# Unused strips at both ends of the partition, so that the large tiles of a transformer block begin at multiples of 256 bytes

## The chip, the cores and the metric

The kernel runs on one core of one Trainium2 chip. The metric is the device time of one execution in microseconds. The profile's span runs from the first to the last instruction of one profiled execution; the device time of a run is somewhat longer than such a span.

## The reference

One layer of a hybrid block over 1024 tokens of width 1024, all in float32: stick-breaking attention with 16 heads of 64, a gated short convolution beside it, a gated merge, and a SwiGLU channel layer with 2816 hidden columns.

```python
mod = silu(c) @ ada_w + ada_b                      # six vectors: sh1, sc1, g1, sh2, sc2, g2
h = rmsnorm(x, ln1_g) * (1 + sc1) + sh1
p = h @ w_in                                       # 1024 x 8192
q, k, v, cb, cc, cx, ga, gb = split(p)
q, k = rmsnorm(q, q_norm_g), rmsnorm(k, k_norm_g)  # per head
y_a = stick_breaking_attention(q, k, v)            # strictly causal, 128-query blocks
y_b = cb * causal_dwconv(cc * cx, conv_w)          # three taps
merged = sigmoid(ga) * (y_a @ w_branch_a) + sigmoid(gb) * (y_b @ w_branch_b)
x = x + g1 * (merged @ w_out)
h = rmsnorm(x, ln2_g) * (1 + sc2) + sh2
f = (silu(h @ w_ffn_gate) * (h @ w_ffn_up)) @ w_ffn_down
out = x + g2 * f
```

Stick-breaking attention: with z = q.k / 8, the weight of key s for query t is sigmoid(z_ts) times the product of 1 - sigmoid(z_tj) over s < j < t.

## The kernel before

Every float32 product is made of three matmuls of the type fp32r: each operand is split into a rounded part ("hi", made by ScalarE) and the rest ("lo", made by VectorE), and hi x hi, hi x lo and lo x hi are added up in PSUM. A matmul has one operand that is loaded into the array (the weights' side; row PEld of the profile) and one that is streamed through it. In the helper `half_prod` (L122 to L129), which makes most products, the weights' split `w` is loaded and the factor `fh`, `fl` is streamed, 512 columns of float32, so 2048 bytes in each partition:

```python
for k in range(4):
    nc.tensor.matmul(ps, wh[:, k, :], fh[:, k, :], start=(k == 0), stop=False)    # L127
    nc.tensor.matmul(ps, wh[:, k, :], fl[:, k, :], start=False, stop=False)       # L128
    nc.tensor.matmul(ps, wl[:, k, :], fh[:, k, :], start=False, stop=(k == 3))    # L129
```

So one product is 12 matmuls. The stages, in the order of time:

- Start (to about 70 us): `x` and its transpose `xts` are loaded, the first modulation is summed up on VectorE (`mod_sum`), and the normed input is split into the four `big` tiles. L290 in `mm_tok` makes v and k from them; here the weights' split is streamed. This lasts to about 165 us.
- Gates (165 to about 570 us): q, the convolution's inputs and the two gates are 20 groups ("gates") of 1024 x 256 columns. Each is one Strassen step: seven half products (`g_prod`), whose streamed factors 0 to 3 lie in `big` tiles and whose factors 4, 5 and 6 are the tiles `ft4`, `ft5` and `ft6`. GpSimd makes the sums of the weights (`ws`), and a generator (`mods_later`) sums the second modulation on VectorE beside the later gates.
- Attention (575 to about 1005 us): scores (L782, L783), sigmoid on ScalarE into `pt`, a scan on VectorE (L788), transposes (L803), and the product with the values' differences (L818, L819). A second generator (`fillers`) puts the products of the convolution branch between (L876 to L878, L895 to L897).
- Merge and output projection (1005 to about 1240 us): `w_branch_a` (L876 to L878 with `ya` streamed), then w_o (L1190 to L1192), where the weights' split `whi`, `wlo` is streamed. `preload_wo` brings five of the eight slices of the first half of w_o ahead, into the pool `wpx`.
- Hidden layer (1240 to about 1640 us): 11 groups, each one Strassen step for the gate and one for the up projection, 22 in all, with seven half products each. The streamed factors are `big` tiles and three pairs of own tiles: `rh2`/`rl2`, `rh6`/`rl6` and `rh3`/`rl3`. The results `c..` are split into `fs` and stored to `d_f`.
- Down projection (1640 us to the end): seven products again (`down`, L1410 to L1412), with the weights' split streamed; `f` is loaded back from `d_f`, and `g2b` and `xo` are loaded for the last sums.

Tiles lie in pools that are stacked from both ends of a partition: a pool with `side="right"` grows down from the far end, the others up from the near end. Pools are opened and closed by stage, so that a later stage's tiles lie where an earlier one's were. At the near end lie the constants; most constants have odd sizes, so the first large tile behind them begins 64 bytes past a multiple of 256, and since the tiles behind it are multiples of 256 bytes long, nearly all have that offset. At the far end the first pool holds `rq` and begins where the partition's usable space ends; nearly all of its followers lie 224 past a multiple of 256. In bytes from the start of the partition:

| tile | at, before | past 256 | past 64 |
|---|---|---|---|
| first of the four `big` | 22,080 | 64 | 0 |
| `ft6` | 112,192 | 64 | 0 |
| `whi`, `wlo` of the gates (first) | 104,000; 95,808 | 64 | 0 |
| `rh6`, `rl6`, `rh3`, `rl3` | 147,008 to 179,776 | 64 | 0 |
| `ft5`, `ft4` | 195,552; 211,936 | 224 | 32 |
| `rh2`, `rl2` | 212,960; 221,152 | 224 | 32 |
| preloaded w_o, `whi`, `wlo` | 207,840; 218,080 | 224 | 32 |
| `pt0` to `pt4` (attention) | 207,840 on | 224 | 32 |
| `c10` to `c31`, `fs` (hidden layer) | 184,288 on | 224 | 32 |
| `dm` (identity), `mk` (mask) | 16,512; 17,024 | 128 | 0 |

The order of instructions on each engine is the program's as the scheduler left it, in part fixed by added dependences (`in_order`, `issue_after`, `high_priority`). Waits between engines are derived from the tiles, including waits for the last user of the bytes in which a new tile comes to lie.

Of the kernel before, what the change touches and what calls it, by code (L numbers as in the profile page):

```python
# [8 lines left out]
F32 = mybir.dt.float32  # L9
# [7 lines left out]
P = 128  # L17
# [6 lines left out]
SECS = (2, 4, 3, 5)  # L24
NH = HID // P
EPS = 1e-6


def block_kernel(tc, x, x_t, cols, ada_1, ada_2, ada_row, w_q, w_kv, w_v1, w_cg, w_a, w_b, w_o, w_g, w_u, w_d, out):
    nc = tc.nc  # L30
    st = ExitStack()
    const = st.enter_context(tc.tile_pool(name="const", bufs=1, reuse_waits="tile"))
# [5 lines left out]
    def nm(s):  # L38
        uid[0] += 1
        return f"{s}_{uid[0]}"  # L40
# [65 lines left out]
    gcol = cst[:, 82:98].rearrange("p (m k) -> p m k", m=2)  # L106
    nc.vector.tensor_scalar(out=qgc, in0=qgc, scalar1=0.125, scalar2=None, op0=ALU.mult)
    mod = const.tile([P, 4, 8], F32, name="mod")
    rqs = ExitStack()
    rqp = rqs.enter_context(tc.tile_pool(name="rqp", bufs=1, side="right", reuse_waits="tile"))  # L110
    rq = rqp.tile([P, 2, 8, H], F32, name="rq")

    def rstd_of(ss, scale, pool, w, r=None, eng=nc.gpsimd):

        m = pool.tile([P, 8], F32, tag="rs_m", bufs=3, name=nm("rs_m"))
        if r is None:
            r = pool.tile([P, 8], F32, tag="rs_r", bufs=3, name=nm("rs_r"))[:, :w]
        eng.tensor_scalar(out=m[:, :w], in0=ss, scalar1=scale, scalar2=EPS, op0=ALU.mult, op1=ALU.add)  # L118
        nc.gpsimd.tensor_tensor(out=r, in0=m[:, :w], in1=nhalf[:, :w], op=ALU.pow)
# [466 lines left out]
    def end_q():  # L586
# [6 lines left out]
        for i in range(8):  # L593
            nc.tensor.transpose(tr[:, i * H:(i + 1) * H], ss[i // 4][:, i % 4 * P:(i % 4 + 1) * P], ident[:H, :H])
        ms = gp.tile([P, 8, H], F32, name="ms16")
        nc.vector.tensor_scalar(out=ms.rearrange("p i h -> p (i h)"), in0=tr[:, :8 * H], scalar1=1.0 / DH, scalar2=EPS,
                                op0=ALU.mult, op1=ALU.add)
# [416 lines left out]
    for n in range(2):  # L1014
        for k in range(KT):
            yr = fp.tile([P, 512], F32, tag="yr", bufs=2, name=nm("yr"))
            nc.sync.dma_start(yr, d_ya[n][:, k, :])
            tag, bufs = slots[n * KT + k]
# [564 lines left out]
```

## Time and profile before

| | us |
|---|---|
| median of 3 runs | 1853.54 |
| lowest, highest | 1847.68, 1854.77 |
| span of the profiled execution | 1845.0 |

The profiled execution's own device time is not told apart from the three; its span lies 2.7 us under the lowest and 8.5 us under the median of the runs. A row of a group names line, engine, operation, the written tile and the tiles read (the streamed one and the loaded one in a matmul, in the order of their names), the shape and the count; behind the bar follow the busy time, the mean duration of one in ns, and the idle time before them. In the timeline each row has the start and the duration in us.

### The profile page before, as it was taken

What the parts mean: (1) busy time and instruction counts of PE and PEld (TensorE: products, weight loads), DVE (VectorE), ACT (ScalarE), POOL (GpSimd) and SP (SyncE); (2) the same over time, 40 slices, a digit from 0 to 9 for tenths busy, and PEclk for the clock granted to TensorE, in tenths of its full rate; (3) what the DMA queues carried; (4) which work ended last, traced back from release to release, by engine and by line L of the source; (5) the groups of instructions that cost most, each with busy time, mean ns of one, the idle gap of its engine ahead of it and who ended that gap; (6) DMA issues with size and microseconds to landing.
All of it is one profiled execution on the core that took longest, in us unless ns stands there. A gap on an engine that the chain in (4) does not pass through costs nothing.

```text
span 1845.0 us, 24888 instructions
## 1 busy us (share of the span) xinstructions
PE 1810.0 (98%) x8829; PEld 1504.7 (82%) x8829; DVE 1346.3 (73%) x1948; ACT 792.1 (43%) x1494; POOL 369.1 (20%) x277
## 2 busy tenths in 40 slices
PE   7999999999999999999999999999999999999999
PEld 5787778888889988888888788877888888878887
DVE  6874776779873888888887644589877787644776
ACT  4352553333343656665665311664443344322321
POOL 1043327423230000000000000115544544200000
PEclk9999999999999999999999999999999999999999
DMA  9598452227748665678554636424533344299766
GB/s 389 196 311 299 166 186 86 80 75 247 273 164 250 158 194 170 188 227 282 154 138 137 211 125 215 137 91 160 194 137 148 139 169 161 103 353 315 283 229 222
DMA packets 147267, 358.01 MB, mean 194 GB/s; under 512 B 15480, under 2 KB 44480, under 8 KB 144968
## 3 DMA queue, kind: packets, MB, share of 16 engines
q1 hardware_dynamic: 101816, 289.12, 46.6%
q10 hardware_dynamic: 44320, 63.64, 10.0%
q0 software_dynamic: 1008, 3.67, 0.5%
q8 instruction: 70, 1.15, 0.3%
q14 instruction: 53, 0.43, 0.1%
HBM read 245.74 MB, written 110.66 MB: 193 GB/s over the span
## 4 chain that ended last, share of the span: by engine, by line
PE 80%; DVE 11%; DMA 5%; issue 2%; ACT 2%; POOL 1%; SPq 0%; ACTq 0%; DVEq 0%; POOLq 0%
PE e L129 7%; PE e L128 7%; PE e L127 7%; PE pj L290 5%; PE pj L127 5%; PE pj L129 5%; PE pj L128 5%; PE pj L876 4%; PE pj L877 4%; PE pj L878 4%; PE e L1411 4%; PE e L1412 4%; PE e L1410 4%; PE tr L803 3%; PE o L819 2%
## 5 line engine op out<-in xcount | busy, mean ns | idle before, releaser
L788 DVE TENSOR_TENSOR_SCAN pt<-pt,mk 128x128 f32<-128x128 f32 (+7 forms) x128 | 172.0, 1350 | 48.2 <-ACT pt L784 48.1
L784 ACT ACTIVATE pt<-z,rq 128x512 f32<-128x512 f32 (+3 forms) x192 | 107.2, 579 | 88.7 <-PE z L783 57.4
L127 PE MATMUL e<-big,whi 128*128 128x512 f32 x352 | 137.4, 390 | 3.6 <-ACT c L1310 2.0
L128 PE MATMUL e<-big,whi 128*128 128x512 f32 x352 | 137.0, 389 | 0.0
L129 PE MATMUL e<-big,wlo 128*128 128x512 f32 x352 | 137.0, 389 | 0.0
L132 DVE TENSOR_TENSOR c<-e,c 128x512 f32<-128x512 f32 x138 | 92.9, 687 | 57.4 <-PE e L129 55.7
L118 POOL TENSOR_SCALAR rs_m<-ss 128x1 f32<-128x1 f32 x8 | 1.7, 218 | 651.0 <-ACT xn L1213 651.0
L127 PE MATMUL pj<-big,whi 128*128 128x512 f32 x320 | 125.1, 391 | 0.4 <-DVE c L132 0.4
L128 PE MATMUL pj<-big,whi 128*128 128x512 f32 x320 | 124.7, 390 | 0.0
L129 PE MATMUL pj<-big,wlo 128*128 128x512 f32 x320 | 124.3, 390 | 0.0
L1410 PE MATMUL e<-whi,f 128*128 128x512 f32 (+1 forms) x319 | 122.2, 384 | 1.8 <-DMA f<-d_f 1.8
L1411 PE MATMUL e<-wlo,f 128*128 128x512 f32 (+1 forms) x319 | 122.5, 384 | 0.0
L1412 PE MATMUL e<-whi,f 128*128 128x512 f32 (+1 forms) x319 | 122.3, 384 | 0.0
L132 DVE TENSOR_TENSOR c<-pj,c 128x512 f32<-128x512 f32 x140 | 93.3, 682 | 31.2 <-PE pj L129 30.9
L290 PE MATMUL pj<-whi,big 128*128 128x512 f32 x352 | 110.9, 401 | 3.1 <-ACT big L273 3.0
L132 DVE TENSOR_TENSOR wlo<-raw,whi 128x512 fp32r<-128x512 f32 x116 | 88.7, 768 | 32.7 <-ACT whi L473 32.6
L473 ACT ACTIVATE whi<-raw 128x512 fp32r<-128x512 f32 x116 | 72.6, 629 | 92.4 <-PE pj L128 38.9
L132 POOL TENSOR_TENSOR ws<-raw,raw 128x512 f32<-128x512 f32 x40 | 56.7, 1417 | 276.5 <-DMA raw<-w_cg 134.6
L807 DVE TENSOR_TENSOR atl<-tr,ath 128x512 fp32r<-128x512 f32 (+1 forms) x192 | 99.6, 548 | 14.4 <-ACT ath L806 12.6
L806 ACT ACTIVATE ath<-tr 128x512 fp32r<-128x512 f32 (+1 forms) x192 | 86.9, 490 | 43.6 <-PE o L818 25.2
L128 PE MATMUL e<-rl,whi 128*128 128x512 f32 x264 | 103.6, 392 | 1.4 <-DVE rl L132 1.4
L876 PE MATMUL pj<-big,whi 128*128 128x512 f32 x256 | 103.9, 406 | 0.0
(255 smaller groups left out, 5017.8 us busy)
## 6 DMA issues: line engine op xcount, KB each, us to landing
f<-d_f SPq DMA_DIRECT2D x77, 512.0 KB, 4.2
d_f<-fs SPq DMA_DIRECT2D x70, 512.0 KB, 3.3
raw<-w_cg SPq DMA_DIRECT2D x40, 512.0 KB, 4.3
raw<-w_u SPq DMA_DIRECT2D x26, 512.0 KB, 3.3
raw<-w_g SPq DMA_DIRECT2D x25, 512.0 KB, 3.5
ad<-ada ACTq DMA_DIRECT2D x19, 512.0 KB, 6.0
ada<-ada SPq DMA_DIRECT2D x8, 1024.0 KB, 10.4
d_t<-ts SPq DMA_DIRECT2D x16, 512.0 KB, 5.2
```

The costliest lines, as they stand in the source:

```text
L127: nc.tensor.matmul(ps, wh[:, k, :], fh[:, k, :], start=(k == 0), stop=False)
L128: nc.tensor.matmul(ps, wh[:, k, :], fl[:, k, :], start=False, stop=False)
L129: nc.tensor.matmul(ps, wl[:, k, :], fh[:, k, :], start=False, stop=(k == 3))
L132: eng.tensor_tensor(out=out, in0=a, in1=b, op=op)
L290: nc.tensor.matmul(ps, a, b, start=(k == 0 and q == 0), stop=(k == KT - 1 and q == 2))
L784: nc.scalar.activation(pt[:, off + s0:off + s0 + m], z[:, :m], AF.Sigmoid, scale=rq[:, 1, i, h:h + 1])
L788: nc.vector.tensor_tensor_scan(out=pt[:, rev], data0=pt[:, rev], data1=mk[:, rev], initial=1.0, op0=ALU.mult, op1=ALU.max)
L807: nc.vector.tensor_tensor(out=tl[:, :nb, c0:c0 + P], in0=src, in1=th[:, :nb, c0:c0 + P].bitcast(F32), op=ALU.subtract)
L876: nc.tensor.matmul(ps, wh, rh_, start=(k == 0), stop=False)
L1410: nc.tensor.matmul(o, sh, w[0][:, c], start=(j == 0), stop=False)
L1411: nc.tensor.matmul(o, sh, w[1][:, c], start=False, stop=False)
L1412: nc.tensor.matmul(o, sl, w[0][:, c], start=False, stop=(j == NJ - 1))
```

## The change

Two tiles are added that no instruction touches: 192 bytes at the end of the near-end constants that are made before the other pools' tiles, and 224 bytes as the first thing at the far end. With them, the near-end tiles listed above begin at a multiple of 256, and so do the far-end tiles: `big` at 22,272, `ft6` at 112,384, `ft5` at 195,328, `ft4` at 211,712, `rh2` at 212,736, `rl2` at 220,928. `dm`, `mk` and the other constants ahead of the strip stay where they are.

```diff
+PADL, PADR = 192, 224
 ...
     mod = const.tile([P, 4, 8], F32, name="mod")
+    const.tile([P, PADL // 4], F32, name="padl")
+    st.enter_context(tc.tile_pool(name="padr", bufs=1, side="right", reuse_waits="tile")).tile(
+        [P, PADR // 4], F32, name="padr")
     rqs = ExitStack()
     rqp = rqs.enter_context(tc.tile_pool(name="rqp", bufs=1, side="right", reuse_waits="tile"))
```

## The prediction

> **What bounds the kernel now.** I read the page first, then the granted clock, the busy time by stretches, the chain of waits of three stretches, and last the timeline of TensorE alone.
>
> ```profile
> span 1845.0 us, 24888 instructions
> PE 1810.0 (98%) x8829; PEld 1504.7 (82%) x8829; DVE 1346.3 (73%) x1948; ACT 792.1 (43%) x1494; POOL 369.1 (20%) x277
> PE 80%; DVE 11%; DMA 5%; issue 2%; ACT 2%; POOL 1%; SPq 0%; ACTq 0%; DVEq 0%; POOLq 0%
> ```
> ```profile
> core 0: 1845.0 us, clock 0.996
> ```
> ```profile
> core 0: us, PE busy (x) PEld busy (x) DVE busy (x) ACT busy (x) POOL busy (x), PEclk, DMA share, GB/s
> 165.00:300.00 135.00, 131.36 (x574) 103.33 (x573) 94.62 (x137) 63.54 (x107) 57.06 (x38) 0.99 0.53 181
> 300.00:413.00 113.00, 113.00 (x495) 92.75 (x494) 80.87 (x119) 35.97 (x59) 48.23 (x32) 1.00 0.24 84
> 413.00:575.00 162.00, 160.97 (x730) 132.58 (x730) 126.44 (x188) 60.46 (x102) 47.46 (x28) 1.00 0.65 222
> 1300.00:1500.00 200.00, 200.00 (x879) 164.87 (x878) 154.90 (x207) 84.88 (x144) 90.70 (x63) 1.00 0.41 153
> 1500.00:1625.00 125.00, 125.00 (x550) 102.97 (x550) 92.82 (x128) 51.08 (x86) 47.65 (x33) 1.00 0.40 147
> ```
>
> TensorE is busy for 98% of the span, at a granted clock of 0.996, and in the stretches 300 to 413 and 1300 to 1625 it has no gap at all. So a transfer or a VectorE instruction that gets shorter is mostly worth nothing; what counts is the distance from one matmul's start to the next, its pace. The mean duration in the groups (389 ns and up) is no pace, since matmuls overlap. The pace is read from the timeline. In the gate stage:
>
> ```profile
> 336.15 0.39 PE L127 MATMUL pj<-big,whi 128*128 128x512 f32 x1
> ...
> 341.59 0.40 PE L127 MATMUL pj<-ft,whi 128*128 128x512 f32 x1
> ...
> 347.21 0.40 PE L127 MATMUL pj<-ft,whi 128*128 128x512 f32 x1
> ...
> 349.94 0.39 PE L127 MATMUL pj<-big,whi 128*128 128x512 f32 x1
> ```
>
> From 336.15 to 341.59 stand 24 matmuls that stream `big` tiles: 5.44 us, 226.7 ns each. From 341.59 to 347.21 stand 24 that stream `ft5` and then `ft4`: 5.62 us, 234.2 ns each. From 347.21 to 349.94 stand 12 on `ft6`: 2.73 us, 227.5 ns. Same line, same shape, same weights' tiles, no gap. The allocation tells them apart: `big`, `ft6` and the weights begin 64 bytes past a multiple of 256; `ft5` and `ft4`, at the far end of the partition, begin 224 past one, which is 32 past a multiple of 64. The hidden-layer stage shows the same with other tiles:
>
> ```profile
> 1389.51 0.39 PE L127 MATMUL e<-rh,whi 128*128 128x512 f32 x1
> ...
> 1392.23 0.40 PE L127 MATMUL e<-rh,whi 128*128 128x512 f32 x1
> ...
> 1395.03 0.39 PE L127 MATMUL e<-rh,whi 128*128 128x512 f32 x1
> ...
> 1397.77 0.39 PE L127 MATMUL e<-big,whi 128*128 128x512 f32 x1
> ```
>
> Twelve on `rh6`/`rl6` (at 64): 2.72 us. Twelve on `rh2`/`rl2` (at 224): 2.80. Twelve on `rh3`/`rl3` (at 64): 2.74, the first few still late.
>
> **The change part by part.** It adds no instruction: two strips that nobody writes or reads. On TensorE, VectorE, ScalarE and GpSimd the built program has the same instructions, operands and shapes in the same order. On SyncE's queue the transfers keep their order, and three waits stand elsewhere: `g2b` now also waits for GpSimd's last count, and the first `xo` for one more of VectorE's and for two `d_f` writes of GpSimd's queue, for which two later `f` loads waited before. Below, GpSimd's last instruction, the landing times of its seven `d_f` writes, and the issues of `g2b` and `xo`:
>
> ```profile
> 1642.90 0.53 POOL L1336 DMA_DIRECT2D d_f<-fs  x1 [1.88 <-DVE fs L132]
> ```
> ```profile
> DMA to landing us min/median/max: 6.7/7.5/8.5
> ```
> ```profile
> L1460 SPq DMA_DIRECT2D g2b<-d_g x1: 319/319/319, 1647.6 to 1647.6; - x1
> L1446 SPq DMA_DIRECT2D xo<-d_x x12: 319/422/987, 1684.3 to 1832.8; - x12
> ```
>
> GpSimd's last instruction starts at 1642.90, before `g2b` at 1647.6; its transfer lands within 8.5 us, by 1651.4, and the first `xo` goes at 1684.3, long after `g2b` was let go by VectorE's count before. So these waits cost nothing; behind them on SyncE would stand the `f` loads, which TensorE needs, but there are 33 us to spare.
>
> What moves is addresses. Every left-hand tile behind `mod` moves up by 192 bytes (64 to 0 past 256), every right-hand tile down by 224 (224 to 0). Few stay off: `xn`, every second `uu`, and the constants `dm` and `mk` ahead of the strip.
>
> Term one, tiles at 224 that TensorE streams. How many:
>
> ```profile
> L127 PE MATMUL pj<-ft,whi 128*128 128x512 f32 x240 | 95.4, 397 | 2.3 <-ACT whi L473 2.3
> L127 PE MATMUL e<-rh,whi 128*128 128x512 f32 x264 | 103.3, 391 | 0.0
> L1190 PE MATMUL e<-whi,big 128*128 128x512 f32 x128 | 49.9, 395 | 0.0
> ```
>
> L128 and L129 have the same counts. Of the three `ft` tiles two are at 224, so each of 20 gates has 24 slow matmuls; `rh2`/`rl2` is one factor of three, 22 products of 12. Of w_o's first half five of eight weight slices (preloaded `whi`, `wlo`) are at 224: 5 slices x 8 token tiles x 3 = 120 matmuls. A gate saves 5.62 - 5.44 = 0.18 and 0.01 of the trail in `ft6`: 0.19 x 20 = 3.8 us. A hidden-layer product saves 2.80 - 2.72 = 0.08 and 0.02 of the trail: 0.10 x 22 = 2.2 us. The 120, at 7.5 ns from the gate row: 0.9 us. Sum 6.9 us.
>
> How much of it reaches the end:
>
> ```profile
> by line: PE pj L127 33.5%; PE pj L128 33.4%; PE pj L129 33.4%
> ```
> ```profile
> by line: PE pj L129 12.2%; PE pj L127 12.1%; PE pj L128 11.9%; DVE ad L537 10.7%; issue 9.8%; DVE c L132 8.5%; DVE uu L537 7.4%; DVE wlo L132 7.2%; DMA d_g<-uu 3.4%; DMA uu<-ada 2.6%; DMA raw<-w_cg 2.5%; POOL ws L132 2.3%; DMA d_sga<-c 1.6%
> ```
>
> The first is the chain of 300 to 413, TensorE alone (1300 to 1500 likewise): all arrives. The second is 413 to 575: TensorE is a third of the chain, VectorE's sums of the second modulation as much. Eight gates lie there, 1.5 us; if VectorE sets the pace, it swallows them. So 5.4 to 6.9; I take 6.0, since TensorE is still busy 160.97 of 162.
>
> This is where the Trainium skill speaks against the change. SBUF — State Buffer, section Specifications (TRN2), names 16-byte cachelines as the unit that costs; 64 and 224 are both multiples of 16, so by it TensorE would gain 0. The timeline's 7.5 ns between them disagree, and the measurement decides.
>
> Term two, the tiles at 64 that go to 0. No row has a streamed tile at 0. The steady pace has a part that isn't columns:
>
> ```profile
> 1838.39 0.28 PE L1411 MATMUL e<-wlo,f 128*128 128x256 f32 x1
> ...
> 1839.11 0.28 PE L1411 MATMUL e<-wlo,f 128*128 128x256 f32 x1
> ```
>
> Six 256-wide matmuls in 0.72 us, 120 ns each; so 256 more columns cost 106.7 ns, 512 cost 213.3, and 226.7 holds 13.3 ns on top. That is the most that alignment could take from each. Nothing excludes a loss either, at most the 7.5 ns of the one bad case known. I take 0: the step between 64 and 224 is about the time of 16 columns (16 x 0.417 = 6.7 ns), which are 64 bytes. A row of 2048 bytes that begins 32 past a multiple of 64 touches 33 pieces of 64 bytes; one at a multiple touches 32, whether at 64 or at 0.
>
> Term three, the other engines and DMA. VectorE shows no price for 224:
>
> ```profile
> L132 DVE TENSOR_TENSOR c<-pj,c 128x512 f32<-128x512 f32 x140 | 93.3, 682 | 31.2 <-PE pj L129 30.9
> L132 DVE TENSOR_TENSOR c<-e,c 128x512 f32<-128x512 f32 x138 | 92.9, 687 | 57.4 <-PE e L129 55.7
> ```
>
> 682 ns with `c` at 64, 687 mostly at 224. GpSimd is 20% busy, so what it gains is hidden. DMA ends TensorE's waits twice in earnest:
>
> ```profile
> PE pj L249 <- DMA xq<-x: 5.2, 2, 4.6
> PE e L1410 <- DMA f<-d_f: 1.8, 1, 1.8
> ```
>
> 7.0 us in all; transfers a few per cent shorter give some 0.2 of it. Bounds: 0.7 us either way. I take 0.
>
> Sum: 6.0 us. The span goes from 1845.0 to 1839.0. The record does not tell which of the three runs was profiled; the span lies 8.5 us under their median of 1853.54, so the forecast is **1847.5 us**, 0.3% less.
>
> **The rivals.** *Every matmul gains (14%).* If 64 is not good enough either, the 13.3 ns or one step of 6.7 go in all stages. Five groups alone:
>
> ```profile
> L127 PE MATMUL e<-big,whi 128*128 128x512 f32 x352 | 137.4, 390 | 3.6 <-ACT c L1310 2.0
> L127 PE MATMUL pj<-big,whi 128*128 128x512 f32 x320 | 125.1, 391 | 0.4 <-DVE c L132 0.4
> L1410 PE MATMUL e<-whi,f 128*128 128x512 f32 (+1 forms) x319 | 122.2, 384 | 1.8 <-DMA f<-d_f 1.8
> L290 PE MATMUL pj<-whi,big 128*128 128x512 f32 x352 | 110.9, 401 | 3.1 <-ACT big L273 3.0
> L876 PE MATMUL pj<-big,whi 128*128 128x512 f32 x256 | 103.9, 406 | 0.0
> ```
>
> All but L290 come three times: 3 x 1247 + 352 = 4093 matmuls, 27 us at 6.7 ns, 54 at 13.3; with the 6.0, 1793 to 1820, say 1807. Against it: 226.7 recurs everywhere at 64, and the rest can as well be a fixed price per matmul. For it: TensorE: Matmul & The Clock Gate, section Back-to-back issue gap, of the Trainium skill gives N/2.4 + 2.5 ns, 215.8 for 512; no row here reaches that.
>
> *Nothing happens (12%).* The slow tiles lie not only at 224 but all above 195,000 bytes of the partition, and no streamed tile lies there at 64. If place and not alignment is slow, nothing changes: 1853.5.
>
> *Slower (7%): like offsets collide.* Before, the hidden-layer stage writes `c` and `fs` at 224 while TensorE reads at 64; after, all begin at 0. If that costs each of its 3 x (352 + 264) = 1848 matmuls the one step of 7.5 ns, it is 13.9 us, and the stage's 2.2 don't come: 1853.5 + 13.9 - 3.8 = 1863.6. It decides from 7.1 ns per matmul. Against it: weights and streamed tile both at 64, like offsets, is the fastest pair of the trace.
>
> *DMA gains more than hidden (7%).* The chain has 5% DMA, 92 us; were a twentieth of that to go, 4.6 us, with the 6.0: 1842.9. DMA: Bandwidth & Descriptors, section How a descriptor splits into AXI transactions, of the Trainium skill has a 4096-byte row at 64 take 17 transactions, at 0 16; no run here shows it. Against it: only 7.0 us of TensorE's waiting is for DMA.
>
> **How the numbers follow.** My forecast has 60%, the rivals 14, 12, 7 and 7. A measurement of this kernel tells about 0.5% from no change (9.3 us; the three runs differ by 7.1). Faster by more: the first rival, 14, most of the DMA one, 5, and the edge of the forecast, 4: 0.23. Slower: the collision, 6, and 2 of the nothing case: 0.08. Within: 0.69. The range leaves out the first rival and the collision, 20%, and takes in nothing, DMA and the spread of the runs: 1836 to 1858.
>
> **What would show it.** Right: `ft5`/`ft4` and `rh2`/`rl2` at 226.7 ns, so that 24 take 5.44 us and each hidden-layer half 0.10 us less; `big` unchanged. `big` under 220 ns makes me wrong to the fast side; `ft` still at 234 makes it place; `big` at 234 in the hidden-layer stage makes it collision.

## The result, and the profile after

The changed kernel takes 1844.49 us (median of 6 runs, 1843.07 to 1846.98), the kernel before on the same chip 1850.69 (median of 6, 1847.68 to 1854.77). The ratio is 0.9975, with a 95% interval of 0.9963 to 0.9987: 6.2 us less. The forecast was 6.0 us less and 1847.5 us; its range was 1836 to 1858.

The profiled execution of the changed kernel took 1843.09 us. Its page and granted clock; the kernel's lines have moved down by four, so L131 to L133 are the L127 to L129 of before, L1196 is L1192 and L1415 is L1411:

```profile
span 1841.3 us, 24885 instructions
PE 1804.7 (98%) x8829; PEld 1502.7 (82%) x8829; DVE 1350.0 (73%) x1948; ACT 792.0 (43%) x1494; POOL 370.3 (20%) x277
core 0: 1841.3 us, clock 0.997
```

TensorE is busy for 5.3 us less (1810.0 before), VectorE for 3.7 us more. The span is 3.7 us shorter. Now the timeline of TensorE at the two places that the prediction read, start and duration in us. First the 36 matmuls of a gate that stream `ft5`, `ft4` and `ft6` (the second row is the first matmul behind them), then the 36 of a hidden-layer half that stream `rh6`, `rh2`, `rh3` and their rests:

```profile
340.51 0.39 PE L131 MATMUL pj<-ft,whi 128*128 128x512 f32 x1
...
348.67 0.39 PE L131 MATMUL pj<-big,whi 128*128 128x512 f32 x1
...
1377.92 0.39 PE L131 MATMUL e<-big,whi 128*128 128x512 f32 x1
...
1388.80 0.39 PE L131 MATMUL e<-rh,whi 128*128 128x512 f32 x1
...
1396.96 0.39 PE L131 MATMUL e<-big,whi 128*128 128x512 f32 x1
```

(The row at 1377.92 begins the 48 matmuls on `big` ahead of the second block.) Both blocks of 36 take 8.16 us, 226.7 ns for each matmul. Before they took 349.94 - 341.59 = 8.35 and 1397.77 - 1389.51 = 8.26. So a gate gives 0.19 us and a half 0.10, as forecast. The `big` tiles have not become faster: 48 matmuls from 1377.92 to 1388.80 are 226.7 ns each.

The same instruction can be followed through both traces. Three of them, each in the kernel before and then in the changed one; the brackets hold the idle time before the instruction and what ended it:

```profile
1180.03 0.39 PE L1192 MATMUL e<-whi,big 128*128 128x512 f32 x1
...
1234.93 0.50 PE L128 MATMUL e<-rl,whi 128*128 128x512 f32 x1 [1.37 <-DVE rl L132]
...
1650.18 0.39 PE L1410 MATMUL e<-whi,f 128*128 128x512 f32 x1
```
```profile
1178.22 0.39 PE L1196 MATMUL e<-whi,big 128*128 128x512 f32 x1
...
1235.20 0.50 PE L132 MATMUL e<-rl,whi 128*128 128x512 f32 x1 [2.48 <-DVE rl L136]
...
1646.40 0.39 PE L1414 MATMUL e<-whi,f 128*128 128x512 f32 x1
```

In the output projection the changed kernel is 1.81 us ahead, at the start of the hidden layer 0.27 us behind, and at the start of the down projection 3.78 ahead. In the hidden layer's first product TensorE waits for VectorE's `rl`, 1.1 us longer than before. What follows shows in the stretches (length; busy time of PE, PEld, DVE, ACT and POOL; granted clock; DMA), before and then after:

```profile
1230.00:1235.00 5.00, 3.63 (x17) 2.67 (x15) 5.00 (x7) 4.04 (x4) 0.00 (x0) 1.00 0.29 105
1235.00:1240.00 5.00, 5.00 (x22) 4.13 (x23) 5.00 (x8) 2.31 (x4) 0.00 (x0) 1.00 0.23 70
1630.00:1650.00 20.00, 20.00 (x83) 16.32 (x83) 7.36 (x12) 4.61 (x8) 2.67 (x5) 0.92 1.00 397
```
```profile
1230.00:1235.00 5.00, 2.13 (x9) 1.20 (x7) 5.00 (x6) 3.79 (x4) 0.00 (x0) 1.00 0.31 105
1235.00:1240.00 5.00, 4.80 (x14) 3.81 (x15) 5.00 (x9) 2.54 (x5) 0.00 (x0) 0.66 0.19 48
1630.00:1650.00 20.00, 20.00 (x90) 16.57 (x89) 5.80 (x10) 3.46 (x6) 2.65 (x5) 1.00 1.01 397
```

VectorE is busy without a gap in both, and there it sets the time. Behind the longer idle time the changed kernel has a stretch at half the clock (a granted clock of 0.66 in the mean of 1235 to 1240), where matmuls start 0.43 us apart; the kernel before has one at 1630 (0.92), which the changed one has not. So the two executions differ by more than their matmuls' paces, and the 3.7 us between their spans are not the work of the change alone.

### The profile page after: what moved, and what is told of

It is laid out like the page before. It is cut to its first block, busy times and chain, and to the rows that moved or that the text cites. A ratio compares the mean times of both kernels' runs of the same rounds, so it can differ in the third digit from the quotient of the medians.

```text
span 1841.3 us, 24885 instructions
## 1 busy us (share of the span) xinstructions
PE 1804.7 (98%) x8829; PEld 1502.7 (82%) x8829; DVE 1350.0 (73%) x1948; ACT 792.0 (43%) x1494; POOL 370.3 (20%) x277
## 4 chain that ended last, share of the span: by engine, by line
PE 73%; DVE 11%; DMA 9%; ACT 3%; issue 3%; POOL 1%; SPq 0%; ACTq 0%; DVEq 0%; POOLq 0%
PE e L132 6%; PE e L131 6%; PE e L133 6%; PE pj L131 5%; PE pj L133 5%; PE pj L132 5%; PE pj L294 5%; PE pj L880 4%; PE pj L881 4%; PE pj L882 4%; PE e L1414 3%; PE e L1416 3%; PE e L1415 3%; PE tr L807 3%; PE o L823 2%
## 5 line engine op out<-in xcount | busy, mean ns | idle before, releaser
L131 PE MATMUL e<-big,whi 128*128 128x512 f32 x352 | 137.2, 390 | 2.2 <-ACT c L1314 2.2
L133 PE MATMUL e<-big,wlo 128*128 128x512 f32 x352 | 137.1, 389 | 0.0
L131 PE MATMUL pj<-big,whi 128*128 128x512 f32 x320 | 125.1, 391 | 0.8 <-DVE c L136 0.8
L132 PE MATMUL pj<-big,whi 128*128 128x512 f32 x320 | 124.7, 390 | 0.0
L133 PE MATMUL pj<-big,wlo 128*128 128x512 f32 x320 | 124.3, 390 | 0.0
L1415 PE MATMUL e<-wlo,f 128*128 128x512 f32 (+1 forms) x319 | 121.8, 382 | 0.0
L807 PE MATMUL tr<-dm,pt 128*128 128x128 f32 x576 | 98.0, 274 | 6.2 <-DVE atl L811 5.6
```

Source lines behind the costliest of these rows:

```text
L807: nc.tensor.transpose(tr[:, j * P:(j + 1) * P], pt[:, off + (b0 + j) * P:off + (b0 + j + 1) * P], ident)
L1415: nc.tensor.matmul(o, sh, w[1][:, c], start=False, stop=False)
```

## The experiments

Three theories of the 7.5 ns were tested. *Pieces*, the prediction's own: a streamed row that begins off a multiple of 64 bytes touches one piece of 64 more. *Place or multiples*: the far end of the partition is slow, or a multiple of 256 is fast. *Pair*: neither tile's offset counts alone; a matmul is slow where the streamed and the loaded tile begin at different offsets within 256 bytes. In the kernel before, `ft5` and `ft4` at 224 run against weights at 64, but all three theories fit that.

All kernels are the one before with the strips of the change at other sizes, unless a diff says otherwise. Times in us; the ratio is to runs of the kernel before on the same chip (medians of before: 1851.7, 1849.83 and 1850.36 in three sessions).

| kernel | near end, far end past 256 | time | ratio, interval |
|---|---|---|---|
| change | 0, 0 | 1844.49 | 0.9975, 0.9963 to 0.9987 |
| change again | 0, 0 | 1843.93 | 0.9972, 0.9960 to 0.9983 |
| `left_only` | 0, 224 | 1851.16 | 0.9996, 0.9985 to 1.0007 |
| `right_only` | 64, 0 | 1850.25 | 0.9990, 0.9977 to 1.0002 |
| `left_at_96` | 96, 0 | 1851.36 | 0.9999, 0.9981 to 1.0016 |
| `right_at_192` | 64, 192 | 1852.07 | 0.9998, 0.9984 to 1.0011 |
| `right_by_160` | 64, 64 | 1844.38 | 0.9972, 0.9960 to 0.9984 |
| `right_by_416` | 64, 64 | 1845.07 | 0.9972, 0.9960 to 0.9983 |
| `loaded_at_32` | 0, 0, weights of the gates 32 | 1854.60 | 1.0021, 1.0008 to 1.0035 |
| `loaded_at_192` | 0, 0, weights of the gates 192 | 1850.53, one run | none |

**One strip alone.** The two halves of the change.

```diff
-PADL, PADR = 192, 224
+PADL, PADR = 192, 0        # left_only: the strip at the near end alone
+PADL, PADR = 0, 224        # right_only: the strip at the far end alone
```

Expected of the near end alone:

> Only the 192 bytes at the near end; far-end tiles stay at 224 past 256. Theory 64: ft5/ft4 and rh2/rl2 stay at 234 ns, everything else at 226.7 ns, time of before within its interval. Theory that multiples of 256 help the other transfers or engines (DMA, ScalarE): about 2 us or more faster than before with the paces unchanged.

Expected of the far end alone:

> Only the 224 bytes at the far end; near-end tiles stay at 64 past 256. Theory 64 (a streamed row of 2048 bytes costs about 7.2 ns more when it does not begin at a multiple of 64 bytes, and nothing else of the alignment matters): ft5/ft4 and rh2/rl2 at 226.7 ns, big at 226.7 ns, time as with both strips, 4 to 6 us under before. Theory pair (streamed and loaded operand must have the same offset within 256 bytes, else 7 ns): ft5/ft4 and rh2 now at 0 with weights at 64, so 234 ns stay and the time is that of before.

Neither is told from the kernel before. The gate's 36 matmuls in the timeline of TensorE, with the near end at 0 and `ft5`, `ft4` still at 224, and then with `ft5`, `ft4` at 0 and the weights still at 64:

```profile
341.80 0.40 PE L129 MATMUL pj<-ft,whi 128*128 128x512 f32 x1
...
350.15 0.39 PE L129 MATMUL pj<-big,whi 128*128 128x512 f32 x1
```
```profile
341.60 0.39 PE L130 MATMUL pj<-ft,whi 128*128 128x512 f32 x1
...
349.94 0.39 PE L130 MATMUL pj<-big,whi 128*128 128x512 f32 x1
```

8.35 and 8.34 us: both as slow as before. The second one fells the prediction's reason. `ft5` and `ft4` begin at a multiple of 256 and touch 32 pieces, and they are slow all the same. Each strip alone is worth nothing; only the two together are.

**Off a multiple of 64, but together.**

```diff
-PADL, PADR = 192, 224
+PADL, PADR = 32, 224       # near-end tiles at 96 past 256, far-end tiles at 0
```

> Near-end strip of 32 bytes instead of 192: nearly all near-end tiles begin 96 past 256, which is 32 past a multiple of 64; far-end tiles at 0. Theory 64: big, whi, f, ya, ft6, rh6 and rh3 now at 234 ns as streamed tiles and ft5/ft4 and rh2 at 226.7 ns; some 5900 matmuls of 512 columns by 7.2 ns are 42 us more than with both strips, so about 37 us (2.0%) slower than before. Theory place (the far end is slow whatever the offset): no change of pace at the near end, time as with both strips. Theory pair: ft5/ft4 (0 with weights at 96) at 234 ns, big (96 with 96) at 226.7 ns.

The timeline of TensorE, 48 matmuls on `big` (at 96, weights at 96) and 36 on the `ft` tiles (`ft5`, `ft4` at 0, `ft6` at 96):

```profile
332.57 0.39 PE L131 MATMUL pj<-big,whi 128*128 128x512 f32 x1
...
343.45 0.40 PE L131 MATMUL pj<-ft,whi 128*128 128x512 f32 x1
...
351.80 0.39 PE L131 MATMUL pj<-big,whi 128*128 128x512 f32 x1
```

The 48 take 10.88 us, 226.7 ns each, though 96 is 32 past a multiple of 64 as 224 is. By the pieces theory they would be slow and the kernel some 37 us longer; they are as fast as any in this study, and the time is that of before. The 36 take 8.35, as slow as before.

**Other distances.** `right_at_192` puts the far end at 192, 128 bytes from the weights' 64. In the other two the changed kernel's tiles stay at 0, and the gates' weights, not the streamed tiles, are moved by a strip in their own pool; the weights of the start and of the convolution branch move with them, those of w_o, the hidden layer and the down projection stay at 0.

```diff
-PADL, PADR = 192, 224
+PADL, PADR = 0, 32         # right_at_192
 
     gw = gws.enter_context(tc.tile_pool(name="wpl", bufs=1, reuse_waits="tile"))
+    gw.tile([P, 8], F32, name="padw")     # loaded_at_32, on the changed kernel
+    gw.tile([P, 48], F32, name="padw")    # loaded_at_192, on the changed kernel
```

> Only 32 bytes at the far end: far-end tiles begin 192 past 256, a multiple of 64 but not of 128 or 256; near-end tiles at 64. Theory 64: ft5/ft4 and rh2/rl2 at 226.7 ns, time as with both strips, 4 to 6 us under before. Theory 128 or 256: 234 ns or some value between stays and the time is nearer to before.

> Both strips as in the change, and 32 unused bytes ahead of the pool of the gates' weights, so that in the start, the gates and the attention stage whi/wlo lie at 32 past 256 while big and ft5/ft4 stay at 0. Theory pair (the pace depends on the difference between the streamed and the loaded operand's offset; 0 gives 226.7 ns, any other about 233.4): big and ft5/ft4 streamed against whi (gates, 1440 matmuls; big in the attention stage, 768) and whi against big in the start (576) all at about 233.4 ns, ft6, which moves along to 32, at 226.7; 2784 x 6.7 ns = 18.7 us more than with both strips, some 13 us (0.7%) over before. Theory 64 (only the streamed operand's own offset counts): only the 576 of the start and ft6 (240) slow, 5 to 6 us more than with both strips, time of before.

> As loaded_at_32, with 192 bytes ahead of the pool: whi/wlo of start, gates and attention at 192 past 256, big at 0. Differences streamed minus loaded are 64 (gates, attention) and 192 (start). Pair theory: about 233 ns for both; theory 64: 226.7 ns everywhere, since every offset is a multiple of 64.

In the timeline of `right_at_192` the gate's 36 matmuls take 8.33 us, nearly as long as before, although 192 is a multiple of 64:

```profile
341.30 0.40 PE L130 MATMUL pj<-ft,whi 128*128 128x512 f32 x1
...
349.63 0.39 PE L130 MATMUL pj<-big,whi 128*128 128x512 f32 x1
```

In `loaded_at_32` and then in `loaded_at_192` the 48 matmuls on `big`, which no other kernel made slow:

```profile
334.26 0.40 PE L131 MATMUL pj<-big,whi 128*128 128x512 f32 x1
...
345.47 0.40 PE L131 MATMUL pj<-ft,whi 128*128 128x512 f32 x1
```
```profile
332.88 0.40 PE L131 MATMUL pj<-big,whi 128*128 128x512 f32 x1
...
343.88 0.39 PE L131 MATMUL pj<-ft,whi 128*128 128x512 f32 x1
```

11.21 us, 233.5 ns each, with the weights 32 above `big`; 11.00 us, 229.2 ns, with the weights 192 above, which is `big` 64 above the weights in the next 256. Moving the loaded tile alone makes the streamed one slow. The pair theory had 233 ns for `loaded_at_192` too, so in size it missed there. In the same two executions the products that stream `ya`, whose tile moves along with its weights to 32 and to 192, stay at 227 ns. Over all traces, outside the attention stage, the mean distance from start to start is, by the streamed tile's offset less the loaded one's, within 256:

| distance | streamed at, loaded at | ns |
|---|---|---|
| 0 | 0, 0; 64, 64; 96, 96 | 226.7 |
| 32 | 32, 0 | 233.1 |
| 64 | 0, 192 | 229.3 |
| 128 | 192, 64 | 232.9 |
| 160 | 224, 64; 0, 96 | 234.0 |
| 192 | 0, 64; 192, 0 | 233.3 |
| 224 | 224, 0; 0, 32 | 233.4 |

No distance is faster than 0. `loaded_at_32` ends 10.1 us above the change's 1844.49 and 10.2 above `right_by_160` of the same session, where 18.7 were expected; its span is 12.2 us longer than the changed kernel's. By the program 2784 of its matmuls of 512 columns have tiles at unlike offsets: 576 at the start, 1440 in the gates and 768 of the convolution branch in the attention stage, at 6.5 ns each 3.7, 9.4 and 5.0 us. Set against the changed kernel's trace, the same matmul starts 1.7 us later at 165 us, 9.9 at 575 and 11.3 at 1005: 1.7 of 3.7 us arrive at the start, 8.1 of 9.4 in the gates, 1.4 of 5.0 in the attention stage. In the attention stage the expectation had the size wrong: the same matmuls stand about 2 ns further apart than in the changed kernel (235 ns there, 237 here), not 6.5, and 2 ns for each of 768 are 1.5 us. TensorE's idle time takes up little: up to 165 us it falls from 12.7 to 12.0 us, and in the attention stage it rises from 7.0 to 7.8. Why unlike offsets cost less in the attention stage was not tested.

**Like offsets that are no multiple of 256.** Only the far end has a strip, of a size that brings its tiles to 64, where the near end's are. With 160 bytes they are 256 apart from the near end's within 512, with 416 equal there too.

```diff
-PADL, PADR = 192, 224
+PADL, PADR = 0, 160        # right_by_160
+PADL, PADR = 0, 416        # right_by_416
```

> Only a far-end strip, of 160 bytes: far-end tiles at 64 past 256, as the near-end ones, but the two ends differ by 256 within 512. Pair theory with a period of 256: ft5/ft4 and rh2/rl2 at 226.7 ns, time as with both strips, 4 to 6 us under before. Pair theory with a period of 512 or more: 233 ns, time of before.

> Only a far-end strip, of 416 bytes: all large tiles at both ends 64 past a multiple of 512, none at a multiple of 256. Pair theory: ft5/ft4 and rh2/rl2 at 226.7 ns and the time of the change, 0.9975 of before. If it is multiples of 256 that matter: 233 ns and the time of before.

Both give the whole gain, 0.9972 of before. The gate's 36 matmuls, with 160 and with 416 bytes:

```profile
340.47 0.39 PE L130 MATMUL pj<-ft,whi 128*128 128x512 f32 x1
...
348.63 0.39 PE L130 MATMUL pj<-big,whi 128*128 128x512 f32 x1
```
```profile
340.22 0.39 PE L130 MATMUL pj<-ft,whi 128*128 128x512 f32 x1
...
348.38 0.39 PE L130 MATMUL pj<-big,whi 128*128 128x512 f32 x1
```

8.16 us in both. Nearly all large tiles lie at 64 past 256 here, the same distance from a multiple as in the kernel before. So it is not the multiple that the change's strips buy, but that both ends agree; and agreeing within 256 is enough. The far end is fast at 64, so the place isn't slow either.

**The two places apart.** 160 bytes behind the two tiles alone, so that they move from 224 to 64.

```diff
     ft = {q: ftp.tile([P, 2, 4, 512], F32R, name=f"ft{q}") for q in (5, 4)}
+    ftp.tile([P, 40], F32, name="padf")        # gates_by_160
 
+            r2p.tile([P, 40], F32, name="padh")    # hidden_by_160, behind rh2 and rl2
```

> The kernel before with 160 unused bytes behind `ft5` and `ft4` alone, so that these two begin 64 past a multiple of 256 like the weights; `rh2`, `rl2` and the preloaded w_o stay at 224. Pair theory: `ft5` and `ft4` at 226.7 ns, `rh2` and w_o at 234 as before; matmuls start 2.0 us earlier at 413 us and 2.4 earlier at 575. If this arrives, the time is 2.4 us (0.13%) under before, ratio 0.9987. Handover theory: the lead is gone at 1240 us, ratio 1.000.

> The kernel before with 160 unused bytes behind `rh2` and `rl2` alone, so that these, and `c10` to `c31` and `fs` behind them, begin 64 past a multiple of 256; `ft5`, `ft4` and w_o stay at 224. Pair theory: `rh2` and `rl2` at 226.7 ns, `ft5`, `ft4` and w_o at 234; 0.10 us less for each of 22 halves, 2.2 us from 1240 to 1640 us, ratio 0.9988. `c` and `fs` at 64, beside tiles that TensorE reads at 64, cost nothing. Rival: VectorE or GpSimd, which write `c` and `fs`, gain or lose by the new place, so that the stage changes by something else than 2.2 us.

Gates alone: 1847.09 us, 0.9982 (0.9973 to 0.9991), 3.3 us under before. Hidden layer alone: 1847.81, 0.9985 (0.9974 to 0.9997), 2.5 us under. The gate's 36 matmuls take 8.16 us in the first and 8.34 in the second:

```profile
341.02 0.39 PE L127 MATMUL pj<-ft,whi 128*128 128x512 f32 x1
...
349.18 0.39 PE L127 MATMUL pj<-big,whi 128*128 128x512 f32 x1
```
```profile
342.17 0.40 PE L127 MATMUL pj<-ft,whi 128*128 128x512 f32 x1
...
350.51 0.39 PE L127 MATMUL pj<-big,whi 128*128 128x512 f32 x1
```

The two together are 5.8 us; the 0.4 to 0.6 left of the change's 6.2 to 6.4 are of the order of w_o's 0.9, but each of these medians is known to about 2 us only. The gates' gain arrives in the medians, so the handover does not swallow all of it.

In single traces the gain can be followed where TensorE does not wait: by how much the same matmul's lead over the kernel before grows within a stretch, in us. (The gates of the two `loaded_at` kernels are left out.)

| stretch | tiles in question | in traces where they agree | change at most, where they don't |
|---|---|---|---|
| 300 to 413, six gates | `ft5`, `ft4` | 1.12 | 0.12 |
| 1080 to 1180, w_o | preloaded `whi`, `wlo` | 0.95 to 1.00 | 0.09 |
| 1300 to 1625, hidden layer | `rh2`, `rl2` | 1.7 | 0.23 (`right_at_192`) |

Between 413 and 575 us no gain can be read. The kernels with agreeing tiles come out between 0.5 us better and 4.1 worse there than before, those with unlike tiles between 0.2 and 4.2 worse. So `gates_by_160`, which was to be 2.0 us ahead at 413 and 2.4 at 575, is 1.3 ahead and then 0.3 behind, and its span is 2.2 us longer than that of before; its loads of `ft5` and `ft4` also stand in the other order. `hidden_by_160` gains 1.95 us from 1240 to 1625, of the 2.2 expected to 1640.

**The handover to the hidden layer.** The changed kernel once more, and with the last subtraction ahead of the split of `rh3`, `rl3` moved from VectorE to GpSimd, which is idle there.

```diff
     for k in (slice(0, 2), slice(2, 4)):
-        tt(nc.vector, h2b[1][0][:, k], h2b[1][0][:, k], h2b[1][1][:, k], ALU.subtract)
+        tt(nc.gpsimd, h2b[1][0][:, k], h2b[1][0][:, k], h2b[1][1][:, k], ALU.subtract)
```

> The changed kernel once more, for a second profiled execution. Pair theory (a matmul is slow when the streamed and the loaded tile begin at different offsets within 256 bytes): all paces 226.7 ns again, time ratio to before 0.9975, about 1845. Handover theory (VectorE sets the time at which the hidden layer begins, near 1235 us, and swallows what was gained up to there): TensorE idles there again for about 3 us, behind `rl`, a half-clock window of 3.4 us follows it, and the starts of matmuls at 1240 us are not ahead of before's, although they were 1.8 us ahead at 1180. Rival, chance: the windows of half clock lie elsewhere in this execution, and at 1240 us the lead is some 3 us, as it was in the kernel with 416 bytes at the far end.

> The changed kernel with one thing more: the two subtractions that make the last of the hidden layer's input sums (`h2b[1][0]` minus `h2b[1][1]`, 2.35 us on VectorE at 1229.85) go to GpSimd, which is idle there. Handover theory: VectorE's queue gets shorter by 2.3 us, `rl` of factor 3 comes some 2 us earlier, TensorE's idle time at 1232 to 1235 falls from 3.1 us to about 1, no half-clock window follows; time 2 to 4 us under the changed kernel, 1841 to 1843. Rival: GpSimd needs 1.31 us for a 128x512 sum, 5.2 us for these; the last split then waits for GpSimd in place of VectorE, and the time is the changed kernel's or up to 3 us more, 1844.5 to 1847.5.

The second execution of the changed kernel shows the same handover: TensorE waits 2.49 us for `rl`, a stretch of half clock follows (6.8 us, not 3.4; the clock in 1235 to 1240 is 0.55), and its matmuls, 0.1 us behind before's at 1180, are 4.2 behind at 1240 and 0.8 at 1300. But its time is 1843.93, 6.4 us under before. In the trace of `right_by_416` the wait is 1.47 us, and the lead of 3.2 us at 1180 is 3.2 at 1240 and 3.4 at 1300. So in the two executions of the changed kernel, which have the longer wait, 0.7 and 1.5 us of the lead are lost there, and with the shorter wait nothing. Whether the kernel's offsets decide it is open: the medians of the kernels don't follow it.

The kernel with the moved subtraction is slower: 1847.72 us, 0.9995 of before (0.9984 to 1.0005) and 3.8 us above the changed kernel's 1843.93 of the same session. In its trace the matmuls fall 2.2 us further behind those of the changed kernel's between 1180 and 1300 us. VectorE's split at this place, in the changed kernel and then in `handover_pool`, and GpSimd's two subtractions there:

```profile
1218.96 2.36 DVE L136 TENSOR_TENSOR big<-h2b,big 128x1024 fp32r<-128x1024 f32 x2 [1.13 <-ACT big L1092]
```
```profile
1219.24 5.84 DVE L136 TENSOR_TENSOR big<-h2b,big 128x1024 fp32r<-128x1024 f32 x2 [1.13 <-ACT big L1092]
1218.24 5.75 POOL L136 TENSOR_TENSOR h2b<-h2b,h2b 128x1024 f32<-128x1024 f32 x2 [12.60 <-DVE h2b L136]
```

While GpSimd works, the same split takes 5.84 us in place of 2.36. 2.3 us taken off VectorE cost it 3.5. The Trainium skill, SBUF — State Buffer, section "SBUF: two separate sides", says that VectorE and GpSimd share one pair of ports, for which a VectorE instruction with two SBUF inputs and a GpSimd instruction that reads SBUF compete, and that one of them holds it for a whole instruction while the other waits. The trace agrees: GpSimd's two instructions end at 1220.65 and 1223.99, and VectorE's two each end 1.1 us later, at 1221.73 and 1225.07, where one alone takes 1.2.

But that is not the whole of the loss. VectorE's split into `rl`, and the wait of TensorE behind which the loss comes, in the changed kernel and then in `handover_pool`:

```profile
1233.93 2.35 DVE L136 TENSOR_TENSOR rl<-h2b,rh 128x1024 fp32r<-128x1024 f32 x2
1271.68 0.50 PE L131 MATMUL e<-big,whi 128*128 128x512 f32 x1 [2.18 <-ACT c L1314]
```
```profile
1233.61 2.34 DVE L136 TENSOR_TENSOR rl<-h2b,rh 128x1024 fp32r<-128x1024 f32 x2
1274.14 0.80 PE L131 MATMUL e<-big,whi 128*128 128x512 f32 x1 [4.84 <-ACT c L1314]
```

`rl` comes 0.3 us earlier, not 2, and TensorE no longer waits for it. At 1270 us the matmuls are only 0.2 us further behind than at 1180; the other 2.0 are lost by 1300, where TensorE waits 4.84 us for ScalarE's `c` in place of 2.18 and 6.8 us of half clock set in. With the subtraction moved, the scheduler also put VectorE's and ScalarE's later work into another order, so what makes that wait longer stays open. The rival's reason, a last split that waits for GpSimd, did not occur: GpSimd was done 9.6 us before it began.

## Why the prediction was right, and where its reason was wrong

- *What bounds the kernel.* Right. TensorE's pace sets the time: of the nine other kernels with several runs that differ from before in little but offsets, the four whose tiles agree in more places and in none fewer (`right_by_160`, `right_by_416`, `gates_by_160`, `hidden_by_160`) have intervals below 1, and no other has.
- *Term one, tiles at 224.* The sizes were right: 0.19 us a gate and 0.10 a hidden-layer half, both measured to the hundredth. w_o's 0.9 shows as the lead's growth between 1080 and 1180 us, 1.0 us, in every trace in which its slices agree with `big`.
- *How much arrives.* 6.0 was taken of 6.9; the medians give 6.2 and 6.4. The place where something is lost was misjudged in part: besides the gates of 413 to 575, which no run settles (traces differ there by up to 4.7 us, the gain in question is 1.5), it is the start of the hidden layer, where VectorE is busy 5.00 of 5 us. The prediction read that stage only from 1300 on and did not list the handover. That the medians came within 0.4 us of 6.0 is in part luck, with intervals of about 2 us to either side.
- *Term two, 64 to 0.* The value, 0, was right, the reason wrong. The step that failed is "A row of 2048 bytes that begins 32 past a multiple of 64 touches 33 pieces". Tiles at 96 run at 226.7 ns against weights at 96, and tiles at 0 run at 233 against weights at 64. By that reason moving the far end alone would have brought the whole gain; measured, it brought 0.9990 (0.9977 to 1.0002) and slow tiles.
- *Term three.* 0 was right within what can be seen: VectorE's busy time rose by 3.7 us in one trace, GpSimd's by 1.2, no gain; and the kernels whose tiles all stay at 64 (`right_by_160`, `right_by_416`) are as fast as the change.
- *The rivals.* "Every matmul gains" fell by `big` at 226.7, "nothing happens" by `ft` at 226.7. "DMA gains more than hidden" finds no support: the strip that leaves the tiles at 64 brings the whole gain, and the near end at 0 alone brings none (0.9996). "Like offsets collide" had the sign of the truth turned round: like offsets are the fast case. The sentence against it, that both operands at 64 are the fastest pair of the trace, was the one that held the mechanism, and it was used only to fend off a rival.
- *The base.* 1847.5 is 3.0 above the measured time because the median of three runs, 1853.54, lay high; over 32 runs before has 1850.36.
- *The rule of 16-byte cachelines* (the Trainium skill, SBUF — State Buffer, section Specifications (TRN2)), by which TensorE would gain 0: every offset of this study is a multiple of 16, and paces still differ by 6.6 ns, so it doesn't say what is fast here.

What is not shown is why unlike offsets cost 6.6 ns. Weights are loaded while matmuls stream (PEld is busy 82% of the span, beside PE), so a clash of the two reads would fit, but every matmul of every run has its own weight load, and none shows the pace without one.

## What to carry to other kernels

Where TensorE is the bound and each matmul comes with a weight load, as in these float32 products, read the distance between starts tile by tile and set it beside both operands' addresses: equal offsets within 256 bytes for the streamed and the loaded tiles gave about 3% of those matmuls' time here, and one strip of 160 bytes at one end did what the change's two did. Before a theory about one tile's alignment is believed, look for a pair in the same trace that has the other operand elsewhere; and move one operand at a time. An idle engine isn't a free one: a sum that GpSimd took over from VectorE made VectorE's next split 2.5 times as long.

## What the hardware showed that was not expected

- The cost of unlike offsets is nearly a step: 6.2 to 7.3 ns at distances of 32, 128, 160, 192 and 224 bytes, but only 2.6 at 64. The period is 256 bytes and not a half or a quarter of it: 256 apart is as fast as 0, but 128 and 64 apart are slow. Distances under 32 were not tried.
- Between 100 and 1800 us the granted clock falls to half for 3.4 us at a time, once to four times in one execution (twice for 6.8 us, in the second execution of the change and in `handover_pool`). The places differ between executions, but not at will: all 31 such stretches of the fourteen traces begin during a wait of TensorE of 1.8 us or more, or within 1.6 us of its end. Of 47 waits of that length 31 have one, so the wait alone does not decide it; shorter waits have none. Matmuls of the changed kernel in the stretch behind the wait of 2.48 us at 1235.20:

```profile
1236.13 0.63 PE L132 MATMUL e<-rl,whi 128*128 128x512 f32 x1
1236.56 0.63 PE L133 MATMUL e<-rh,wlo 128*128 128x512 f32 x1
1236.99 0.63 PE L131 MATMUL e<-rh,whi 128*128 128x512 f32 x1
```

They start 0.43 us apart in place of 0.227; one stretch costs about 1.7 us, as much as nine gates gain by the change. This is one part of what lets one profiled span stand for little here: the two spans of the same changed kernel are 1841.3 and 1842.7, those of the two kernels at 64 are 1845.0 and 1837.7, at medians 0.6 and 0.7 us apart. Of the 7.3 us between the last two, one such stretch at 520 us is 1.7; most of the rest also arises between 413 and 1005 us, where TensorE waits for other engines.
